# Storing the first three blocks of a layer norm + GELU kernel tile by tile instead of block by block

## The chip, the cores and the metric

One core of one Trainium2 chip. The metric is the device time of one execution in microseconds (us). A profile is of one execution; its span is some 1.7 us shorter than the execution's time.

## The reference

```python
x: (8, 1024, 2048) float32; gamma, beta: (2048,) float32; eps = 1e-5
mean = np.mean(x, axis=-1, keepdims=True)
var = np.var(x, axis=-1, keepdims=True)
normalized = (x - mean) / np.sqrt(var + eps)
out = gamma * normalized + beta
return 0.5 * out * (1 + np.tanh(np.sqrt(2 / np.pi) * (out + 0.044715 * out ** 3)))
```

67.1 MB are read and 67.1 MB written, and each element is touched once, so little can beat the rate of the transfers.

## The kernel before

The 8192 rows are 64 tiles of 128 rows (1 MB each). Block 0 is tile 0 alone; blocks 1 to 21 have three tiles (3 MB each). A block has one input buffer, there are seven, GELU writes back into it, and the block is stored from it. The load of block b + 7 is emitted behind the store of block b, because it takes the same buffer.

```python
NB = 7
starts = [0] + list(range(1, ntiles, R))                  # R = 3
def rows(ap, b):
    return ap[rows_of[b]].rearrange("(p k) d -> p k d", p=P)
def load(b):
    xt = xin.tile([P, R, d], F32, name="xt")              # pool of NB buffers
    src = rows(xf, b); m = src.shape[1]
    if b < 2:
        for k in range(m):
            nc.sync.dma_start(out=xt[:, k, :], in_=src[:, k, :])      # L68
    else:
        nc.sync.dma_start(out=xt, in_=src)                            # L70
    # ... (cut)
```

With `(p k) d`, partition p holds three rows that lie next to each other in memory. A whole block therefore moves as one run of 24 KB per partition, a single tile as one run of 8 KB.

```python
def gelu(j):
    g, k = of_tile[j]
    b, q = block_of[j]
    dst = rows(of, b)
    last = b >= len(starts) - 3
    for h, (pt, s) in enumerate(zip(ps[j % 2], halves)):
        nc.scalar.activation(out=xts[j][:, s], in_=pt, func=ACTF.Gelu_apprx_tanh,
                             scale=rstds[g][0][:, k:k + 1])           # L178
        if j == ntiles - 1:
            nc.scalar.dma_start(out=dst[:, q, s], in_=xts[j][:, s])
    if last:
        if j < ntiles - 1:
            nc.scalar.dma_start(out=dst[:, q, :], in_=xts[j])
    elif q == dst.shape[1] - 1:
        nc.scalar.dma_start(out=dst, in_=blocks[b][:, :dst.shape[1], :])
        if b + NB < len(starts):
            load(b + NB)
```

Loads are issued by SyncE (queue q1 in the profile), stores by ScalarE (queue q10), which also does the GELU, a third of the statistics and the scaled diagonals for the matrix products.

Of the kernel before, what the change touches and what calls it, by code (L numbers as in the profile page):

```python
# [19 lines left out]
def kernel(  # L20
# [10 lines left out]
    nc = tc.nc  # L31
# [3 lines left out]
    ntiles = n // P  # L35
# [12 lines left out]
    xts, blocks = {}, {}  # L48


    starts = [0] + list(range(1, ntiles, R))
# [7 lines left out]
# [4 lines that stand above are left out]
        xt = xin.tile([P, R, d], F32, name="xt")  # L63
        src = rows(xf, b)
        m = src.shape[1]
# [6 lines that stand above are left out]
            xts[starts[b] + k] = xt[:, k, :]  # L72
        blocks[b] = xt
# [98 lines left out]
    def gelu(j):  # L172
        g, k = of_tile[j]
        b, q = block_of[j]
        dst = rows(of, b)
        last = b >= len(starts) - 3
        for h, (pt, s) in enumerate(zip(ps[j % 2], halves)):
            nc.scalar.activation(out=xts[j][:, s], in_=pt, func=ACTF.Gelu_apprx_tanh,  # L178
                                 scale=rstds[g][0][:, k:k + 1])
            if j == ntiles - 1:  # L180
                nc.scalar.dma_start(out=dst[:, q, s], in_=xts[j][:, s])
        if last:
            if j < ntiles - 1:
                nc.scalar.dma_start(out=dst[:, q, :], in_=xts[j])
        elif q == dst.shape[1] - 1:
            nc.scalar.dma_start(out=dst, in_=blocks[b][:, :dst.shape[1], :])
            if b + NB < len(starts):
                load(b + NB)

# [7 lines left out]
    for j in range(ntiles):  # L197
        g, k = of_tile[j]
        target = min(len(chunks), max(pos, done_at[g] + AFTER[k]))
        while pos < target:  # L200
            i, c = chunks[pos]
            chunk(i, c)
            pos += 1
            h = of_tile[i][0]
            if done_at[h] == pos:
                while passes and of_tile[passes[0][1]][0] <= h:
                    f, q = passes.pop(0)
                    f(q)
                group_chain(h)
        if k == 0:  # L210
            for q in range(groups[g]):
                diagonal(j + q)
        affine(j)
        if j > 0:
            gelu(j - 1)
        now = of_tile[chunks[min(pos, len(chunks) - 1)][0]][0]
        if passes and of_tile[passes[0][1]][0] <= now and k != 1:
            f, q = passes.pop(0)
            f(q)
    gelu(ntiles - 1)  # L220


# [33 lines left out]
```

## Time and profile before

| | before |
|---|---|
| time, median of the first 3 runs | 319.91 us (319.67 to 320.07) |
| span of the profiled run | 317.9 us |
| busy: PE, VectorE, ScalarE | 80%, 84%, 76% |
| bytes moved, mean rate | 134.38 MB, 423 GB/s |
| transfer engines, slices 2 to 39 of 40 | 90% busy or more each |

It is read so: no compute engine is near full over the span (VectorE comes closest: 203.91 us of the middle 220), while the 16 transfer engines (DMA) are busy for 90% or more in all but the first and the last slice. The prediction below shows the lines.

### The profile page before, as it was taken

What the parts mean: (1) busy time and instruction counts of PE and PEld (TensorE: products, weight loads), DVE (VectorE), ACT (ScalarE), POOL (GpSimd) and SP (SyncE); (2) the same over time, 40 slices, a digit from 0 to 9 for tenths busy, and PEclk for the clock granted to TensorE, in tenths of its full rate; (3) what the DMA queues carried; (4) which work ended last, traced back from release to release, by engine and by line L of the source; (5) the groups of instructions that cost most, each with busy time, mean ns of one, the idle gap of its engine ahead of it and who ended that gap; (6) DMA issues with size and microseconds to landing.
All of it is one profiled execution on the core that took longest, in us unless ns stands there. A gap on an engine that the chain in (4) does not pass through costs nothing.

```text
span 317.9 us, 2209 instructions
## 1 busy us (share of the span) xinstructions
PE 255.8 (80%) x528; PEld 104.1 (33%) x528; DVE 266.1 (84%) x344; ACT 242.6 (76%) x282; POOL 91.2 (29%) x181
## 2 busy tenths in 40 slices
PE   5987979978989889789789895777979595979920
PEld 2322434323433333333233332332423232424400
DVE  2678889999999999999999979797979879797600
ACT  2365989998898988988988969587787769685720
POOL 0203324414225144043142250404234150506000
PEclk9997979999999999999999999979799998979985
DMA  7999999999999999999999999999999999999996
GB/s 292 436 442 442 387 438 422 428 429 430 436 431 433 430 433 433 427 436 431 427 433 439 430 430 432 433 431 436 424 436 433 436 425 433 430 439 409 426 429 265
DMA packets 7649, 134.38 MB, mean 423 GB/s; under 512 B 850, under 2 KB 850, under 8 KB 1106
## 3 DMA queue, kind: packets, MB, share of 16 engines
q1 hardware_dynamic: 3456, 67.11, 49.5%
q10 hardware_dynamic: 4180, 67.13, 49.3%
q8 instruction: 4, 0.07, 0.1%
q14 instruction: 9, 0.07, 0.1%
HBM read 67.13 MB, written 67.11 MB: 422 GB/s over the span
## 4 chain that ended last, share of the span: by engine, by line
DMA 42%; DVE 31%; issue 9%; POOL 5%; PE 4%; ACT 4%; ACTq 0%; POOLq 0%; DVEq 0%; SPq 0%
DMA out_dram<-xt 26%; DVE ps L166 17%; DMA xt<-in_x_dram 16%; DVE st L125 13%; PE ps L169 4%; ACT xt L178 3%; DVE mv L127 1%; POOL y L149 1%; ACT w L160 1%; POOL t L152 1%; ACT junk L131 1%; POOL ve L148 1%; POOL t L151 1%; POOL y L153 1%; POOL t L150 0%
## 5 line engine op out<-in xcount | busy, mean ns | idle before, releaser
L169 PE MATMUL ps<-b_t,w 128*128 128x512 f32 x512 | 241.8, 626 | 44.4 <-DVE ps L166 38.9
L166 DVE SCALAR_TENSOR_TENSOR ps<-xt,mv,g_t 128x1024 f32<-128x1024 f32 x128 | 156.2, 1265 | 7.0 <-ACT xt L178 6.9
L169 PEld LDWEIGHTS ps<-b_t,w 128*128 128x128 f32 x512 | 99.0, 199 | 188.0 <-issue 102.3
L178 ACT ACTIVATE xt<-ps,y 128x1024 f32<-128x1024 f32 x128 | 137.3, 1104 | 25.9 <-PE ps L169 24.9
L125 DVE BATCH_NORM_STATS2 st<-xt 128x6 f32<-128x512 f32 x172 | 107.9, 680 | 23.3 <-DMA xt<-in_x_dram 23.3
L138 POOL TENSOR_SCALAR mv<-sq 128x1 f32<-128x1 f32 x21 | 8.7, 416 | 144.5 <-ACT junk L136 144.5
L136 ACT ACTIVATE junk<-xt,mv 128x2048 fp8e5<-128x2048 f32 x21 | 42.0, 2002 | 8.0 <-ACT xt L178 8.0
L131 ACT ACTIVATE junk<-xt 128x2048 fp8e5<-128x2048 f32 x21 | 40.0, 1904 | 8.4 <-DMA xt<-in_x_dram 7.9
L149 POOL TENSOR_TENSOR y<-ve,power 128x3 f32<-128x3 f32 (+1 forms) x22 | 34.7, 1577 | 1.8
L148 POOL TENSOR_SCALAR ve<-mv 128x3 f32<-128x3 f32 (+1 forms) x22 | 20.2, 918 | 45.5 <-DVE mv L127 45.3
L160 ACT ACTIVATE w<-ident,std 128x128 f32<-128x128 f32 x64 | 20.8, 388 | 7.1 <-POOL std L154 7.1
L127 DVE BATCH_NORM_AGGREGATE mv<-st 128x2 f32<-128x24 f32 x43 | 11.3, 263 | 2.7
L98 PE MATMUL ps<-g_t,ones 1*128 1x512 f32 x8 | 7.2, 1073 | 3.7 <-DMA g_t<-in_gamma_dram 3.7
L101 ACT ACTIVATE g_t<-ps 128x1024 f32<-128x1024 f32 x2 | 2.0, 1023 | 6.7 <-PE ps L98 6.7
L98 PE MATMUL ps<-b_t,ones 1*128 1x512 f32 x8 | 7.0, 1056 | 0.0
L152 POOL TENSOR_SCALAR t<-t 128x3 f32<-128x3 f32 (+1 forms) x22 | 6.3, 287 | 1.9
L151 POOL TENSOR_TENSOR t<-t,ve 128x3 f32<-128x3 f32 (+1 forms) x22 | 6.1, 276 | 1.7
L153 POOL TENSOR_TENSOR y<-y,t 128x3 f32<-128x3 f32 (+1 forms) x22 | 5.2, 235 | 1.8
L101 ACT ACTIVATE b_t<-ps 128x1024 f32<-128x1024 f32 x2 | 2.0, 1023 | 4.8 <-PE ps L98 4.8
L150 POOL TENSOR_TENSOR t<-y 128x3 f32<-128x3 f32 (+1 forms) x22 | 5.1, 234 | 1.7
L154 POOL TENSOR_TENSOR std<-ve,y 128x3 f32<-128x3 f32 (+1 forms) x22 | 4.3, 194 | 1.7
L98 PEld LDWEIGHTS ps<-g_t,ones 1*128 1x128 f32 x8 | 2.5, 325 | 6.8 <-issue 6.8
(12 smaller groups left out, 13.0 us busy)
## 6 DMA issues: line engine op xcount, KB each, us to landing
xt<-in_x_dram SPq DMA_DIRECT2D x20, 3072.0 KB, 22.5
out_dram<-xt ACTq DMA_DIRECT2D x18, 3072.0 KB, 34.9
out_dram<-xt ACTq DMA_DIRECT2D x9, 1024.0 KB, 18.3
xt<-in_x_dram SPq DMA_DIRECT2D x4, 1024.0 KB, 8.6
out_dram<-xt ACTq DMA_DIRECT2D x2, 512.0 KB, 12.1
g_t<-in_gamma_dram ACTq DMA_DIRECT2D x1, 8.0 KB
b_t<-in_beta_dram ACTq DMA_DIRECT2D x1, 8.0 KB
```

Of the source, the lines that this page charges most:

```text
L98: nc.tensor.matmul(pt[:, c:c + BANK], lhsT=ones[0:1, :], rhs=row[0:1, s.start + c:s.start + c + BANK], start=True, stop=True)
L125: nc.vector.bn_stats(out=sts[i][:, c, :], in_=xts[i][:, c * BANK:(c + 1) * BANK])
L127: nc.vector.bn_aggr(out=slot(i), in_=sts.pop(i))
L131: nc.scalar.activation(out=junk, in_=xts[i], func=ACTF.Identity, scale=-1.0 / d, accum_out=slot(i)[:, 0:1], saturate=False)
L136: nc.scalar.activation(out=junk, in_=xts[i], func=ACTF.Square, bias=slot(i)[:, 0:1], accum_out=sq, saturate=False)
L148: po.tensor_scalar(out=ve, in0=mvs[g][:, :, 1], scalar1=float(eps), scalar2=None, op0=ADD)
L149: po.tensor_tensor(out=y, in0=ve, in1=power[:, :m], op=mybir.AluOpType.pow)
L152: po.tensor_scalar(out=t, in0=t, scalar1=-0.5, scalar2=1.5, op0=MUL, op1=ADD)
L160: nc.scalar.activation(out=w, in_=ident, func=ACTF.Identity, scale=rstds[g][1][:, k:k + 1])
L166: nc.vector.scalar_tensor_tensor(out=pt, in0=xts[j][:, s], scalar=mvs[g][:, k, 0:1], in1=g_t[:, s], op0=ADD if j in on_scalar else SUB, op ...
L169: nc.tensor.matmul(pt[:, c:c + BANK], lhsT=wts[j], rhs=b_t[:, s.start + c:s.start + c + BANK], start=False, stop=True, skip_group_check=True)
L178: nc.scalar.activation(out=xts[j][:, s], in_=pt, func=ACTF.Gelu_apprx_tanh, scale=rstds[g][0][:, k:k + 1])
```

## The change: intent and diff

The whole-block store of block 1 cannot leave before its third tile is done, at about 44 us. Single tiles can leave from about 35 us on. The intent is an earlier start of the stores, and with it buffers that come free earlier.

```diff
-        last = b >= len(starts) - 3
+        single = not 3 <= b < len(starts) - 3
...
-        if last:
-            if j < ntiles - 1:
-                nc.scalar.dma_start(out=dst[:, q, :], in_=xts[j])
-        elif q == dst.shape[1] - 1:
-            nc.scalar.dma_start(out=dst, in_=blocks[b][:, :dst.shape[1], :])
+        if single and j < ntiles - 1:
+            nc.scalar.dma_start(out=dst[:, q, :], in_=xts[j])
+        if q == dst.shape[1] - 1:
+            if not single:
+                nc.scalar.dma_start(out=dst, in_=blocks[b][:, :dst.shape[1], :])
             if b + NB < len(starts):
                 load(b + NB)
```

(In the last three blocks `b + NB` is past the end, so the load's new place changes nothing there.)

## The prediction

> **What bounds the kernel now.** I read the head of the page first: the slices of the span, then the time of DMA issues to landing.
>
> ```profile
> span 317.9 us, 2209 instructions
> ...
> DMA  7999999999999999999999999999999999999996
> GB/s 292 436 442 442 387 438 422 428 429 430 436 431 433 430 433 433 427 436 431 427 433 439 430 430 432 433 431 436 424 436 433 436 425 433 430 439 409 426 429 265
> DMA packets 7649, 134.38 MB, mean 423 GB/s; under 512 B 850, under 2 KB 850, under 8 KB 1106
> ...
> xt<-in_x_dram SPq DMA_DIRECT2D x20, 3072.0 KB, 22.5
> out_dram<-xt ACTq DMA_DIRECT2D x18, 3072.0 KB, 34.9
> ```
>
> The transfers are busy 90% or more in every slice but the first and the last. A 3 MB store takes a median 34.9 us to land, though 3.15 MB at 432 GB/s is 7.3 us alone and 14.6 us when it shares the engines half and half. So the median store stands some 20 us in line behind other stores. VectorE is busy 84% of the span and ScalarE 76%; both work ahead of the stores.
>
> Second, the windows of the span (columns: window, length, busy us of five engines with counts, clock, DMA share, GB/s).
>
> ```profile
> 0.00:4.00 4.00, 0.33 (x1) 0.36 (x2) 0.17 (x1) 1.49 (x2) 0.54 (x6) 1.00 0.49 164
> 8.00:30.00 22.00, 18.65 (x24) 7.00 (x23) 16.19 (x25) 10.67 (x14) 5.21 (x15) 0.96 1.03 441
> 30.00:34.00 4.00, 4.00 (x8) 1.62 (x7) 2.89 (x5) 3.54 (x5) 0.00 (x0) 0.78 1.02 393
> 34.00:38.00 4.00, 4.00 (x11) 1.72 (x10) 4.00 (x6) 4.00 (x5) 1.16 (x3) 1.00 0.96 410
> 48.00:52.00 4.00, 4.00 (x11) 1.82 (x10) 3.95 (x5) 3.33 (x5) 3.00 (x6) 1.00 0.95 406
> 60.00:280.00 220.00, 182.94 (x398) 74.61 (x396) 203.91 (x266) 184.94 (x218) 71.09 (x135) 0.98 1.00 432
> 312.00:318.00 6.00, 0.00 (x0) 0.00 (x0) 0.00 (x0) 0.00 (x0) 0.00 (x0) 0.50 0.51 208
> ```
>
> For 220 us in the middle 432 GB/s flow, at a DMA share of 1.00. The span is then nearly a sum: 134.38 MB / 432 GB/s = 311.1 us; the head (first 4 us at 164 GB/s) loses 4 x (1 - 164/432) = 2.5 us; the tail (last 6 us at 208) loses 3.1 us. That is 316.7 of 317.9 us. Where the stores begin, between 30 and 52 us, there are small dips: 4 x (1 - 393/432) = 0.36, 4 x (1 - 410/432) = 0.20 and 4 x (1 - 406/432) = 0.24 us, some 0.8 us in all. That is all that this change could fill, as it acts from about 34 us on.
>
> Third, how loads and stores share the engines. Two windows of the DMA queues: q1 is the load queue, q10 the store queue (packets, MB, share). The first has the 1 MB store of tile 0 beside 3 MB loads, the second only 3 MB transfers.
>
> ```profile
> DMA packets 192, 3.02 MB, mean 432 GB/s; under 512 B 15, under 2 KB 15, under 8 KB 15
> ...
> q1 hardware_dynamic: 96, 2.36, 78.2%
> q10 hardware_dynamic: 96, 0.66, 22.5%
> ```
>
> ```profile
> q10 hardware_dynamic: 494, 10.81, 50.3%
> q1 hardware_dynamic: 485, 10.74, 49.9%
> ```
>
> Packets alternate one for one in both (96 to 96; 494 to 485). A row of a block is one packet of 24 KB, a row of a single tile one of 8 KB, so a single tile's store beside block loads gets a quarter of the bytes, and the sum still reaches 432 GB/s.
>
> Fourth, the chain that ended last and the waits of the load queue.
>
> ```profile
> 209.48 44.87 DMA out_dram<-xt
> 254.37 0.03 SPq L70
> 254.40 0.03 issue
> 254.43 22.49 DMA xt<-in_x_dram
> ```
>
> ```profile
> SPq L70 <- DMA out_dram<-xt: 237.3, 15, 33.8
> ...
> SPq L70 <- DMA xt<-in_x_dram: 6.4, 2, 4.3
> ```
>
> A load goes out when the store of the block seven before it has landed: 15 waits, 237.3 us. A slot comes free only as fast as stores drain, and they drain at the rate of the DMA engines.
>
> **What the Trainium skill says.** In "DMA: Bandwidth & Descriptors", section "Queues, rings and completion order", each DMA engine goes round-robin between the queues that have work, packet by packet. The trace agrees: 96 packets against 96, 2.36 MB against 0.66. The same page, section "Issuing engines are not separate DMA queues", says that transfers started from different engines run on the same 16 DMA engines and interleave; here the pure loads from 8 to 30 us make 441 GB/s and the mixed stretch 432, so starting stores sooner takes the bytes from loads. Its section "Where 436 GB/s comes from" puts the ceiling at 435 GB/s; 432 leaves nothing to win. And "Rules for kernel authors" asks for at least 1 MiB in a transfer, which single tiles still have.
>
> **The change part by part.** Removed: the two 3 MB stores of blocks 1 and 2. Added: six 1 MB stores, so four issues more on ScalarE's queue. Bytes: the same. Tile 0 was stored alone already; the last three blocks are unchanged; the test for the load is only moved in the text, and it still waits for all of a block's stores.
>
> ```profile
> 32.51 2.10 ACT L178 ACTIVATE xt<-ps,y 128x1024 f32<-128x1024 f32 x2
> ...
> 36.48 2.11 ACT L178 ACTIVATE xt<-ps,y 128x1024 f32<-128x1024 f32 x2
> ...
> 42.37 2.09 ACT L178 ACTIVATE xt<-ps,y 128x1024 f32<-128x1024 f32 x2
> 44.49 0.37 ACTq L186 DMA_DIRECT2D out_dram<-xt  x1
> 44.92 2.00 ACT L136 ACTIVATE junk<-xt,mv 128x2048 fp8e5<-128x2048 f32 x1 [0.45 <-ACT xt L178]
> ```
>
> These are the three tiles of block 1. Its first two tiles now go out at about 34.7 and 39 us, ten and six us ahead of the block's issue at 44.49. An issue leaves ScalarE idle 0.45 us, so four more cost 4 x 0.45 = 1.8 us of ScalarE between 34 and 57 us. This lies beside the transfers.
>
> What the early issue brings, worked out with the shares above. From the timeline, tile 0's store goes out at 30.17 us and the load that waits for it at 45.53; 1.05 MB in 15.4 us shows the quarter share. Until about 45 us the store queue is busy with tile 0 before and after, and tiles 1 and 2 only stand behind it. At 45 us some 6.3 MB of loads are left (the last prefetched block and the one just issued; my count of load packets to that time). At three quarters of 432, 324 GB/s, they take 19.4 us, to about 64.5 us. In that time the stores move 19.4 x 108 = 2.1 MB: tiles 1 and 2 and nothing of tile 3. Then the load queue is dry, tile 3 goes at full rate in 2.4 us, to 67 us, and with a landing of about 2 us the next load is issued at 67 to 69 us. Before, it was at 65.6. So the slot comes free no earlier, rather 1 to 3 us later, while the loads are ahead by about 7 us of theirs. The store queue then holds tiles 4 to 6 (issued by 57 us, 3.1 MB, 7.3 us alone), which cover the pause until loads flow again at about 72 us. The next load (before: 80.0 us) follows at 80 to 83 us, and the cadence of 14.5 us, two times 3.15 MB at 432, is back.
>
> Sum: bytes 0; dips between 44 and 52 us, now mixed without a break, -0.2; two new changes between pure and mixed traffic, +0.1 to +0.3; 64 more completion packets (4 transfers of 16), nothing visible; ScalarE's 1.8 us, hidden. Together 0.0 us, give or take 0.5.
>
> **The rivals.** (a) Earlier stores fill the start and free slots sooner. For it: all dips lie there. Against: they sum to 0.8 us, and the engines already run at 393 to 441 GB/s then. It makes 319.1 us at best. (b) The quarter share keeps slots waiting and, with the load queue dry from 64 to 72 us, the store queue dries too. For it: the store queue is short so early. Against: 4.2 MB of stores are issued and undone at 64 us, 9.7 us at full rate, against a pause of 7 to 8 us. If it fails, 1 to 3 us without transfers: 321 to 323. (c) The issues hold ScalarE. In the waits, the load queue waited 6.4 us for earlier loads, so an issue can stand behind an older transfer; stores in quick succession might hold ScalarE some us in the same way, and VectorE behind it. Against: the line of stores that builds up, some 20 us, must first be eaten up, and the last 512 KB stores land 12.1 us after their issue where 1.2 us would move them. So it costs 0 us, or 1.8 if I have the slack wrong: 321.7.
>
> **Range and chances.** The main case leaves the median where it is, 319.8 us (319.91 with -0.1 for the dips). The three runs before lie within 0.4 us. Rival (a) sets the low side and some of (b) the high: 318.9 to 321.0. Two per cent would be 6.4 us, eight times the dips, or twice the worst of (b): faster 0.01, slower 0.02, same 0.97.
>
> **What would show it.** Right: the middle 220 us again at 432 GB/s and a DMA share of 1.00; in the DMA queues between 46 and 62 us equal packets and some 75% to 25% of the share; the load queue empty and only stores for several us after 64; the load of the block after next issued at 67 to 69 us and not before 65; ScalarE's four added idle pieces without a mark in the end. Wrong: a slice after the second with a DMA digit under 9, loads issued well before 65.6 us, stores of 8 KB rows running at half share beside loads, or a 3 MB-store time to landing that falls near 15 us, which would mean that the store line is gone and the compute sets the end.

## The result, and the profile after

| | before | after |
|---|---|---|
| median of 6 runs | 319.81 us (319.66 to 320.38) | 319.91 us (319.79 to 320.33) |
| ratio | | 1.0002, 95% interval 0.9989 to 1.0015 |

A ratio is the mean time of one kernel's runs over that of the other's runs of the same rounds, so it is not quite the ratio of the medians. Executions over 1.5% slower than the fastest of the same kernel are left out of the means. The time is the same.

The head of the page of the changed kernel, and its times from issue to landing:

```profile
span 318.1 us, 2217 instructions
...
DMA  7999999999999999999999999999999999999996
GB/s 296 450 426 436 390 427 429 437 411 442 437 431 426 423 442 436 420 430 440 430 433 426 436 436 433 420 436 439 430 426 436 436 431 426 430 436 413 426 429 263
DMA packets 8225, 134.38 MB, mean 422 GB/s; under 512 B 914, under 2 KB 914, under 8 KB 1170
...
xt<-in_x_dram SPq DMA_DIRECT2D x20, 3072.0 KB, 23.8
out_dram<-xt ACTq DMA_DIRECT2D x16, 3072.0 KB, 37.6
out_dram<-xt ACTq DMA_DIRECT2D x15, 1024.0 KB, 20.9
```

The bytes are the same and the same slices are full. There are 576 packets more (8225 against 7649): 512 because each of the 128 partition rows of two blocks became three, and 64 completions (4 transfers of 16). A 3 MB store still stands in line for most of its 37.6 us. The long middle window of the changed kernel runs at the same rate:

```profile
60.00:280.00 220.00, 184.78 (x396) 75.65 (x395) 203.44 (x264) 183.31 (x214) 72.00 (x136) 0.96 1.01 432
```

Now the start, where the change acts. ScalarE's timeline of the changed kernel (start, length, engine and line; in brackets the idle time before):

```profile
34.70 0.37 ACTq L184 DMA_DIRECT2D out_dram<-xt  x1
35.11 2.00 ACT L136 ACTIVATE junk<-xt,mv 128x2048 fp8e5<-128x2048 f32 x1 [0.45 <-ACT xt L179]
...
39.24 0.34 ACTq L184 DMA_DIRECT2D out_dram<-xt  x1
39.63 1.91 ACT L131 ACTIVATE junk<-xt 128x2048 fp8e5<-128x2048 f32 x1 [0.42 <-ACT xt L179]
```

The first two tiles of block 1 do leave at 34.7 and 39.2 us, ten and five us before the whole block did. What they then get of the engines is in the DMA queues from 46 to 62 us, first of the kernel before, then of the changed kernel (packets, MB, share of the engines):

```profile
q1 hardware_dynamic: 166, 3.69, 55.8%
q10 hardware_dynamic: 131, 3.15, 45.7%
```

```profile
q1 hardware_dynamic: 231, 5.26, 76.6%
q10 hardware_dynamic: 223, 1.70, 25.0%
```

In the changed kernel the packets are again one for one (231 to 223), but the stores' are a third of the size, so they move 1.70 MB where they moved 3.15. The loads gain what the stores lose: 5.26 MB for 3.69. Then, from 64 to 72 us, the loads of the changed kernel have run dry:

```profile
DMA packets 468, 3.34 MB, mean 418 GB/s; under 512 B 63, under 2 KB 63, under 8 KB 63
...
q10 hardware_dynamic: 451, 3.30, 97.7%
q1 hardware_dynamic: 16, 0.02, 0.8%
```

97.7% of the engines go to stores: there were enough of them in line to fill the gap, at 418 GB/s. Over the first 64 us as a whole the queues moved this, before and after:

```profile
q1 hardware_dynamic: 1370, 21.74, 81.1%
q10 hardware_dynamic: 303, 4.51, 16.6%
```

```profile
q1 hardware_dynamic: 1424, 23.04, 85.7%
q10 hardware_dynamic: 437, 3.20, 11.9%
```

The sum is the same, 26.28 and 26.26 MB. Loads gained 1.30 MB and stores lost 1.31, although two of three stores were issued sooner; by 90 us each queue is back within 0.1 MB of the kernel before. Last, the issue of the two loads that wait for blocks 1 and 2, in SyncE's timeline, before and after:

```profile
65.63 0.33 SPq L70 DMA_DIRECT2D xt<-in_x_dram  x1
...
80.01 0.33 SPq L70 DMA_DIRECT2D xt<-in_x_dram  x1
```

```profile
68.18 0.33 SPq L70 DMA_DIRECT2D xt<-in_x_dram  x1
...
83.47 0.33 SPq L70 DMA_DIRECT2D xt<-in_x_dram  x1
```

The buffers come free 2.6 and 3.5 us *later* than before, although the first two tiles of each block left earlier. (The last tile, which frees the buffer, leaves no sooner than the whole block did: at 45.12 us for 44.49, and at 57.55 for 56.71.)

### The profile page after: what moved, and what is told of

Same layout as the page of the kernel before. It is cut to its first block, busy times and chain, and to the rows that moved or that the text cites. A ratio compares the mean times of both kernels' runs of the same rounds, so it can differ in the third digit from the quotient of the medians.

```text
span 318.1 us, 2217 instructions
## 1 busy us (share of the span) xinstructions
PE 256.9 (81%) x528; PEld 104.6 (33%) x528; DVE 266.2 (84%) x344; ACT 242.7 (76%) x282; POOL 91.3 (29%) x181
## 2 busy tenths in 40 slices
DMA packets 8225, 134.38 MB, mean 422 GB/s; under 512 B 914, under 2 KB 914, under 8 KB 1170
## 4 chain that ended last, share of the span: by engine, by line
DMA 42%; DVE 31%; issue 9%; POOL 5%; PE 4%; ACT 4%; ACTq 0%; POOLq 0%; DVEq 0%; SPq 0%
DMA out_dram<-xt 26%; DMA xt<-in_x_dram 17%; DVE ps L166 17%; DVE st L125 13%; PE ps L169 4%; ACT xt L179 3%; DVE mv L127 1%; POOL y L149 1%; POOL t L151 1%; ACT w L160 1%; ACT junk L131 1%; POOL t L150 1%; POOL ve L148 1%; POOL t L152 0%; POOL y L153 0%
## 5 line engine op out<-in xcount | busy, mean ns | idle before, releaser
L179 ACT ACTIVATE xt<-ps,y 128x1024 f32<-128x1024 f32 x128 | 137.2, 1104 | 26.5 <-PE ps L169 24.7
L131 ACT ACTIVATE junk<-xt 128x2048 fp8e5<-128x2048 f32 x21 | 40.0, 1905 | 8.3 <-DMA xt<-in_x_dram 6.6
L149 POOL TENSOR_TENSOR y<-ve,power 128x3 f32<-128x3 f32 (+1 forms) x22 | 33.8, 1537 | 1.8
L151 POOL TENSOR_TENSOR t<-t,ve 128x3 f32<-128x3 f32 (+1 forms) x22 | 7.9, 361 | 1.7
L150 POOL TENSOR_TENSOR t<-y 128x3 f32<-128x3 f32 (+1 forms) x22 | 6.8, 310 | 1.7
L152 POOL TENSOR_SCALAR t<-t 128x3 f32<-128x3 f32 (+1 forms) x22 | 4.3, 197 | 1.9
L153 POOL TENSOR_TENSOR y<-y,t 128x3 f32<-128x3 f32 (+1 forms) x22 | 4.3, 195 | 1.8
## 6 DMA issues: line engine op xcount, KB each, us to landing
out_dram<-xt ACTq DMA_DIRECT2D x16, 3072.0 KB, 37.6
```

Source lines behind the costliest of these rows:

```text
L131: nc.scalar.activation(out=junk, in_=xts[i], func=ACTF.Identity, scale=-1.0 / d, accum_out=slot(i)[:, 0:1], saturate=False)
L149: po.tensor_tensor(out=y, in0=ve, in1=power[:, :m], op=mybir.AluOpType.pow)
L151: po.tensor_tensor(out=t, in0=t, in1=ve, op=MUL)
```

## The experiments

Twelve kernels ran; "the kernel before" was run again beside each. The theory to test (A): the transfer engines are full from 8 us on, so earlier stores only take bytes from loads, and a line of stores covers what ScalarE loses. The first rival (B): a gain and a loss are both there and cancel by chance. Others came up on the way. By the rule that a change under 2% counts as the same, e2, e9 and e12 below are the same as the kernel before and e11 is unclear; where I call one slower all the same, its 95% interval leaves out 1.

### Each block's part alone

```diff
-        single = not 3 <= b < len(starts) - 3
+        single = not 2 <= b < len(starts) - 3            # e3: blocks 0 and 1
+        single = b in (0, 2) or b >= len(starts) - 3     # e4: blocks 0 and 2
```

> Blocks 0 and 1 tile by tile, block 2 whole again. Theory A: the load that waits for block 1's store is issued at 67 to 69 us as in the changed kernel (quarter share until the loads run dry), the next one at about 80 to 82 us in place of the changed kernel's 83.5, for block 2's rows of 24 KB then share half and half; total 319 to 321 us.

> Block 1 whole, block 2 tile by tile. Theory A: the load that waits for block 1's store goes out at 65 to 66 us as in the kernel before, the next one later than that kernel's 80.0, at 83 to 90 us, since block 2's 8 KB rows then have a quarter share beside two loads; total 319 to 321 us.

One run each (state unknown): 319.81 and 320.14 us, beside 319.87 of the kernel before. SyncE's timelines, of e3 and then of e4:

```profile
67.99 0.33 SPq L70 DMA_DIRECT2D xt<-in_x_dram  x1
...
78.88 0.33 SPq L70 DMA_DIRECT2D xt<-in_x_dram  x1
```

```profile
64.76 0.33 SPq L70 DMA_DIRECT2D xt<-in_x_dram  x1
...
83.40 0.33 SPq L70 DMA_DIRECT2D xt<-in_x_dram  x1
```

Each delay belongs to the block that was made single, and only to it: block 1 single gives 68.0 us for the first load, block 2 single 83.4 for the second. Two of the four times lie outside the forecast, by 1.1 us (78.9 for 80 to 82) and 0.2 us (64.8 for 65 to 66), both to the early side.

### The quarter share taken away

```diff
-        if b < 2:
+        if b < 2 or 5 <= b <= 8:          # load(): these blocks, too, tile by tile
```

> The changed kernel, but the loads of blocks 5 to 8, those that run beside the single-tile stores, also go tile by tile, so both queues have packets of 8 KB and share half and half. Theory A: the load that waits for block 1's store is issued earlier than the changed kernel's 68.2 us, at about 57 to 62, and the total stays at 319.9 within 0.5%. Rival B (the late slot costs something that the early store wins back): with the late slot cured the gain shows, 317 to 319 us.

321.05 us (320.45 to 321.87), ratio 1.0037 (1.0025 to 1.0049). SyncE's timeline of this run:

```profile
55.30 1.62 SPq L68 DMA_DIRECT2D xt<-in_x_dram  x2
```

The two issues in it go out at 55.30 and, by the record of the single instructions, 56.59 us; the second is the first tile of the load that waits for block 1, 11.6 us before the changed kernel's 68.18 and just ahead of the forecast (57 to 62). (The other two tiles of that load go out at 66.3 and 66.7 us.) From 40 to 56 us the two queues now share half and half, 50.2% and 50.6%. So the short rows beside long ones did delay the buffer: with rows of the same length the delay is gone. But the time does not fall, it rises by 0.4%, which lies inside the forecast of 0.5%. Rival B, which wanted 317 to 319, is not borne out; as this run has a cost of its own, the stronger evidence against B is the equal sum of bytes in the first 64 us above. Where the cost comes from is shown only in part: between 30 and 40 us 378 GB/s flow in this run, 406 in the changed kernel, worth 10 x (406 - 378)/432 = 0.65 us. A second candidate, whose effect on the end is not shown: ScalarE issued the last store of block 2 at 61.5 us, not at 57.6 as in the changed kernel. That store signals its completion on a semaphore (a counter on which engines wait) that a load issued at 40.9 us also uses, and it went out when that load had landed (at 61.4 us). This kind of wait comes back below.

### Where the transfer engines do have idle time: four buffers

```diff
-    NB = 7
+    NB = 4          # e5 in the kernel before, e6 in the changed kernel
```

> The kernel before with four input buffers in place of seven, the base for the next run. The prefetch then ends at about 28 us and the DMA engines must wait for slots: transfers idle in the first 60 us, and a slot's cycle (load, wait, compute, store, landing) of some 60 to 70 us over four slots gives 15 to 17.5 us a block: 330 to 375 us.

> The changed kernel with four buffers. Theory A (the change is worth nothing only because the DMA engines have no idle time to fill at the start): here they have, single tiles meet no loads and land at once, so block 1's slot comes free some 5 us sooner and the time falls by 1 to 6 us against the four-buffer kernel before. Rival D (earlier issue is worth nothing in itself, as the slot always waits for the last tile): the same within 1 us.

e5: 397.36 us (396.31 to 398.74), more than the 330 to 375 expected; I had taken a buffer's cycle for too short: from 72.81 to 347.00 us a block took 18.3 us, not 15 to 17.5. e6: 394.46 us (392.03 to 395.23). Against the kernel before of the same rounds the ratios are 1.2422 (1.2390 to 1.2453) and 1.2316 (1.2275 to 1.2357): the change wins 0.9% here, and no run of one overlaps a run of the other. (The profiled run of e6, 392.03 us, is its fastest.) The window from 30 to 60 us of e5, then of e6:

```profile
30.00:60.00 30.00, 25.46 (x57) 10.41 (x56) 26.95 (x35) 27.68 (x33) 8.22 (x17) 0.99 0.80 309
```

```profile
30.00:60.00 30.00, 25.19 (x56) 10.26 (x55) 26.43 (x34) 26.49 (x32) 7.96 (x17) 0.98 0.92 364
```

With four buffers the transfer engines are busy for 0.80 of this stretch before the change and 0.92 after: early tiles fill idle time when there is some. SyncE's timeline shows what becomes of it, e5 first, then e6 (the loads that wait for blocks 1 and 2, and the last load):

```profile
53.67 0.33 SPq L70 DMA_DIRECT2D xt<-in_x_dram  x1
...
72.81 0.33 SPq L70 DMA_DIRECT2D xt<-in_x_dram  x1
...
347.00 0.33 SPq L70 DMA_DIRECT2D xt<-in_x_dram  x1
```

```profile
52.46 0.33 SPq L70 DMA_DIRECT2D xt<-in_x_dram  x1
...
68.50 0.33 SPq L70 DMA_DIRECT2D xt<-in_x_dram  x1
...
342.81 0.33 SPq L70 DMA_DIRECT2D xt<-in_x_dram  x1
```

Block 2's buffer comes free 4.3 us sooner, and the last load still goes out 4.2 us sooner. (I had expected the gain at block 1, which gives 1.2.) So the change is not worthless in itself: with seven buffers it has nothing to fill.

### Where compute sets the end: half stores

```diff
-    nc.scalar.dma_start(out=dst, in_=blocks[b][:, :dst.shape[1], :])
+    nc.scalar.dma_start(out=dst[:, :, :H], in_=blocks[b][:, :dst.shape[1], :H])   # blocks 3 to 18
```

This leaves half of those blocks' output unwritten, a wrong result. (The line is e8's; e7's edit does the same for blocks 3 to 18.) e7 is the kernel before with it, e8 the changed kernel.

> The kernel before, but blocks 3 to 18 store only the left half of their columns (a wrong result on purpose), which takes 25 MB or 58 us from the DMA engines, so that compute sets the end. VectorE's 12.47 us a group from 48 us on puts the last issue some 10 us sooner: 299 to 303 us. It is the base for the next run.

> The changed kernel with the same half stores (wrong result on purpose). Theory A with the hidden cost as predicted: ScalarE's four issues of 0.42 us, 1.7 us, are no longer covered by the line of stores and show in part, 0.5 to 2 us slower than the half-store kernel before. Rival C (they cost nothing even there, since ScalarE is not the bound): the same within 0.3 us. Rival B: faster, by 1 us or more, from the earlier start.

e7: 296.22 us (295.95 to 296.47), under the 299 to 303 expected, ratio 0.9255 (0.9240 to 0.9271). e8: 297.05 us (296.83 to 297.06), ratio 0.9282 (0.9269 to 0.9296). The changed kernel is 0.8 us slower; the runs do not overlap, the intervals touch. In the middle of e7 VectorE is busy 207.66 of 210 us and the transfers have room (0.91):

```profile
60.00:270.00 210.00, 181.97 (x406) 73.96 (x404) 207.66 (x271) 184.31 (x219) 77.37 (x135) 1.00 0.91 369
```

That is the hidden cost of the four added issues. ScalarE loses 4 x 0.42 = 1.7 us, and half of it reaches the end when compute sets it. In the two traces GELU lags by 0.5 us in e8 once the four issues are past, at 64 us, and its last piece still does (290.13 for 289.67 us). In the real kernel it lies behind the line of stores.

### The change carried to every block

```diff
-        single = not 3 <= b < len(starts) - 3
+        single = True
```

> Every block is stored tile by tile: 36 more issues in all than the changed kernel has over its own blocks 3 to 18 (48 stores of 1 MB in place of 16 of 3 MB). Theory A (the 16 DMA engines are the bound from 8 us to the last stores, so the order and the size of the transfers only share out the same 432 GB/s): 319.9 us, within 0.5%, a DMA share of 1.00 in the middle, although the loads run at three quarters of the bytes while a store is beside them and then pause for several us in each block. Rival B (gain of earlier stores and cost of slots freed later cancel in the changed kernel by chance): the two do not cancel when repeated 16 times, so the time moves by 3 us or more, either way. Rival C (ScalarE's issue time counts): 32 more issues x 0.42 us = 13 us of ScalarE; if a third of it shows, 324 us.

338.89 us (337.60 to 341.37), ratio 1.0616 (1.0579 to 1.0652). Theory A, as I had put it ("the order and the size of the transfers only share out the same rate"), falls: transfers of the same bytes can cost 19 us. (B had asked for 3 us or more here and got it in number, but the traces below show other effects than B's two.) ScalarE's waits for transfers in this run:

```profile
ACT junk L136 <- DMA out_dram<-xt: 19.6, 7, 3.8
ACT xt L179 <- DMA xt<-in_x_dram: 18.1, 2, 11.6
...
ACT xt L179 <- DMA out_dram<-xt: 3.2, 1, 3.2
ACT junk L131 <- DMA xt<-in_x_dram: 2.7, 1, 2.7
ACT junk L131 <- DMA out_dram<-xt: 0.9, 1, 0.9
```

44.5 us together, with the 0.4 us of each issue, where the changed kernel has 6.6 (its own wait for data). GELU (L179) works on a tile that is long in its buffer, so it needs none of these transfers. Its longest wait, in ScalarE's timeline, and SyncE's timeline shortly before:

```profile
252.02 2.10 ACT L179 ACTIVATE xt<-ps,y 128x1024 f32<-128x1024 f32 x2
265.28 0.34 ACTq L184 DMA_DIRECT2D out_dram<-xt  x1
265.72 1.11 ACT L179 ACTIVATE xt<-ps,y 128x1024 f32<-128x1024 f32 x1 [11.60 <-DMA xt<-in_x_dram]
```

```profile
249.60 0.33 SPq L70 DMA_DIRECT2D xt<-in_x_dram  x1
```

The tile is done at 254.1 us, but its store goes out at 265.28. In the instruction records all transfers of the program signal on eight completion semaphores, which are given out in turn. The store at 265.28 has number 99, and so has the load of 249.60; just ahead of the store stands a wait on that very semaphore, which ends at 265.2. So the store waited for an unrelated load, and everything behind it on ScalarE with it. By the same records all twelve of these waits are of this kind, and the changed kernel has none. With 65 stores in place of 33 (32 more, not the 36 of the expectation), such meetings are frequent.

Two windows of the same run show the rest:

```profile
60.00:270.00 210.00, 156.39 (x327) 62.51 (x325) 172.23 (x222) 150.61 (x175) 53.65 (x112) 0.94 1.01 422
290.00:334.00 44.00, 36.58 (x83) 14.92 (x81) 33.79 (x40) 34.07 (x40) 12.90 (x23) 1.00 0.71 291
```

Up to 270 us the engines are full but move 422 GB/s, not 432. From 290 us on the line of stores is gone and the transfers wait for compute (0.71); in the last 12 us the packet records show all 16 engines at work or none. Both cost time: the first 210 x (1 - 422/432) = 4.9 us, most of the rest is compute that came late. I had three explanations left: ScalarE's issue time (C), its standing behind older transfers (E), and the transfer engines themselves with short rows (F).

### Telling the three apart

e9 gives ScalarE the time of the issues without any transfer:

```diff
+        if not single and q < 2:
+            for _ in range(2):
+                nc.scalar.activation(out=tiny, in_=ones[:, 0:1], func=ACTF.Gelu_apprx_tanh)
```

> The changed kernel with 64 tiny activations (one element per partition, about 0.2 us each as the one in the prologue) after the first two tiles of each of blocks 3 to 18: about 13 us of ScalarE more, the size of the 32 issues that the all-single kernel added, but no transfer more. Theory E (the all-single kernel lost its 19 us by ScalarE standing behind older transfers whose semaphore its next store uses, with 8 semaphores for all transfers): 319.5 to 321.5 us. Rival C (ScalarE's issue time): 327 us or more.

320.35 us (319.73 to 321.28), ratio 1.0013 (0.9992 to 1.0034). ScalarE is busy 251.2 us, for 242.7 in the changed kernel: 8.5 us more, not the 13 that I meant. By rival C, with e1's 19 us for 13, that should cost 12 us; it costs 0.4. Rival C falls: ScalarE's time alone vanishes behind the line of stores.

e10 stores blocks 3 to 18 as two tiles and one, e11 has nine single blocks:

```diff
+        if not single and q == 1:                                                   # e10
+            nc.scalar.dma_start(out=dst[:, :2, :], in_=blocks[b][:, :2, :])
-                nc.scalar.dma_start(out=dst, in_=blocks[b][:, :dst.shape[1], :])
+                nc.scalar.dma_start(out=dst[:, 2, :], in_=xts[j])
-        single = not 3 <= b < len(starts) - 3
+        single = not 9 <= b < len(starts) - 3                                       # e11
```

> Blocks 3 to 18 are stored as two tiles and one tile, 16 issues more than the changed kernel where the all-single kernel had 32. Theory E: in flight in the middle are some 37.6/14.5 x 2 = 5.2 stores and 1.6 loads, under 8, so ScalarE waits little for transfers (under 10 us against that kernel's 44 us in its waits), and the time is 319.5 to 323 us. Rival C (cost in proportion to the issues): half of 19 us, 329 us. Rival F (rows shorter than the loads' 24 KB cost rate, as the 420 GB/s of that kernel's middle hints): about 322 to 324 us with few waits.

> The change carried three times as far: blocks 0 to 8 tile by tile. Theory E with the slack of the store line: ScalarE loses some 10 to 20 us to issues and waits by 130 us, which eats most of the line of some 20 us but does not go through it: 319.5 to 322 us, with a 3 MB store's time to landing well under the changed kernel's 37.6 us. If loss were in proportion to the blocks made single (6 of the 16 that cost 19 us): 327 us.

e10: 328.65 us (327.27 to 329.43), ratio 1.0265 (1.0237 to 1.0293). e11: 326.94 us (324.02 to 327.85), ratio 1.0191 (1.0135 to 1.0246). Both are misses for E as I had put it. Both hit the forecasts of a loss in proportion to the added stores (329 and 327 us): e1, e10 and e11 lose 0.59, 0.54 and 0.58 us for each of 32, 16 and 12. Why the price is so even stays open; ScalarE's issue time is not it (e9), and the traces show different losses. In e10 I had expected under 10 us of such waits; there are 42.4:

```profile
ACT junk L136 <- DMA xt<-in_x_dram: 37.9, 11, 5.2
...
ACT junk L131 <- DMA out_dram<-xt: 4.5, 1, 4.5
```

Counting transfers in flight was the wrong measure: a semaphore comes round in a fixed turn, and a store meets whatever holds its number, here mostly the latest load, however few are in flight in all. In e11 there are four such waits, 15.6 us in all (9.0 before GELU's line, 6.6 of the 8.9 before L131), the last at 142 us. They did not reach the end by way of idle transfers: the engines' share is 1.01 from 60 to 270 us and 0.99 from 270 to 316. The windows from 60 to 270 us of e10 and of e11, and the last 8 us of e11's transfers:

```profile
60.00:270.00 210.00, 166.29 (x346) 66.01 (x345) 178.69 (x230) 158.41 (x188) 56.19 (x115) 0.95 1.01 424
```

```profile
60.00:270.00 210.00, 175.03 (x370) 71.73 (x369) 190.74 (x245) 171.06 (x201) 63.94 (x128) 0.93 1.01 427
316.50:324.50 8.00, 0.00 (x0) 0.00 (x0) 0.00 (x0) 0.00 (x0) 0.00 (x0) 0.51 0.15 62
```

The rate is lower again while the engines are full, and at e11's end most of the 16 engines are done while, by the packet records, one works alone from about 322 to 324.5 us. The 16 engines had come apart. (In e10 they had not: there the share is 0.79 and 0.62 in the last two stretches of 10 us, 300 to 320, and in the end all 16 stop and start together, as in e1.) In the changed kernel the last engine is done at 316.6 us, 2.5 us after the first. This points to F, so the last run asks for it alone: as many issues as the changed kernel, 3 MB each, but in rows of 8 KB.

```diff
-                nc.scalar.dma_start(out=dst, in_=blocks[b][:, :dst.shape[1], :])
+                nc.scalar.dma_start(out=of[rows_of[b]].rearrange("(k p) d -> p k d", p=P), in_=blocks[b])
```

> The changed kernel with as many issues as it has, but the whole-block stores of blocks 3 to 18 go out in rows of 8 KB in place of 24 KB (each block's three tiles land in swapped rows of the output: a wrong result on purpose). Theory E (the loss of the all-single kernel is ScalarE's standing behind older transfers, which comes with the number of transfers): no such waits, 432 GB/s or nearly in the middle, 319.5 to 321.5 us. Theory F (the loss is the transfer engines' own: rows of 8 KB beside rows of 24 KB lower the rate or set the 16 engines apart): 420 to 427 GB/s in the middle, or a last store that lands many us after its issue, and 323 to 330 us with ScalarE waiting for no transfer.

324.45 us (322.73 to 326.91), ratio 1.0161 (1.0129 to 1.0192), rows swapped. ScalarE waits for no transfer but its own data (6.3 us). Its window from 60 to 270 us, and the transfers' end:

```profile
60.00:270.00 210.00, 177.68 (x381) 72.25 (x380) 198.49 (x257) 179.13 (x211) 66.43 (x129) 0.96 1.01 428
315.70:319.70 4.00, 0.00 (x0) 0.00 (x0) 0.00 (x0) 0.00 (x0) 0.00 (x0) 0.50 0.20 82
```

So with no store added and no such wait, the short rows of 16 blocks cost 1.6%. Whether it takes the loads' long rows beside them, no run tests. The profiled run is the fastest of the six (322.73 us). It shows a rate of 428, worth 210 x (1 - 428/432) = 1.9 us, and a long end. How the rest of the 5 us of the median comes about, and why the runs differ by 4 us, no profile here shows. The swapped rows also lie elsewhere in memory, which I could not take apart from their length. Of e1's 19 us, then, some 5 go with short rows (if e12 carries over) and the rest fits the late compute that the semaphore waits bring; that split is argued, not shown, because no run takes those waits away while it keeps the transfers.

## Why the prediction was right

- **"The transfers are the bound, so bytes over rate give the time."** Right for this change: 432 GB/s over the middle 220 us before and after, the same full slices, ratio 1.0002. The first 64 us move 26.28 and 26.26 MB. As a general rule it was too wide: e1, e10, e11 and e12 move the same bytes and take 1.6 to 6.2% longer. One reading beside it was loose: the 441 GB/s of the pure loads, above the ceiling that it cites, comes with a share of 1.03 (a window counts a packet's whole time where it starts), and 441/1.03 is 428. So pure loads are not shown to be faster than mixed traffic.
- **"A single tile's store beside block loads gets a quarter of the bytes."** Right: 25.0% and 76.6% between 46 and 62 us; e2, with equal rows, took the effect away.
- **"The slot comes free no earlier, rather 1 to 3 us later."** Right: 68.18 for 65.63 (forecast 67 to 69), and step by step: by the packet records tile 3 was moved by 66.8 us (forecast 67). Its landing took 1.3 us more; the 2 us of the forecast stand on no line shown. The second was forecast at 80 to 83 and came at 83.47. The reason for the half microsecond: block 2's last tile met the next load and went packet for packet with it again (76 to 82 packets from 72 to 78 us, of 8 and 24 KB), which the working had left out.
- **"The load queue is dry from 64 to 72 us, and the stores in line cover it."** Right: 97.7% of the engines on stores, 418 GB/s.
- **"Dips between 44 and 52 us, -0.2."** Wrong, and small: from 44 to 52 us the rate is 419 before and 418 after. The dip that I saw from 48 to 52 us followed four microseconds at 432; I had read a fluctuation of a short window as a loss.
- **"ScalarE's 1.8 us, hidden."** Right: 0.42 to 0.45 us an issue; e8 shows 0.8 us of it once compute sets the end, and e9 hides five times as much.
- **Rival (c), "an issue can stand behind an older transfer".** It did not matter in this change (no store of the changed kernel waited so), but it is real: e1 has 44.5 us of it.

## What to carry to other kernels

Where the transfer engines are full, an earlier store wins nothing: it takes its bytes from the loads, and a buffer that is freed by the last tile of a block is freed no sooner. Test an "earlier" change by asking what is idle at that moment; with four buffers something was, and the same edit won 0.9%. And don't carry a harmless edit on without measuring: two more blocks in short stores cost nothing, eight cost 1.9%, all of them 6.2%.

## What the Trainium skill lacked or had wrong

- "DMA: Bandwidth & Descriptors", "Queues, rings and completion order": it tells the round-robin by packet, and the trace agrees, but not what follows for the bytes. Here a packet is one row's run, so the queue with 8 KB rows gets 25.0% beside 24 KB rows (231 to 223 packets, 5.26 to 1.70 MB).
- The same page, "Rules for kernel authors", asks for at least 1 MiB in a transfer for full bandwidth. Size alone does not settle it here: 3 MiB stores in 8 KB rows beside 24 KB loads took 1.6% longer, at 428 for 432 GB/s in the middle (the rows also lay elsewhere in memory), and 1 MiB stores in all blocks ran at 422.
- The same page, "Why a DMA increments its semaphore by 16 and not by 1" (and "Dedicate one sem" in the rules): it warns of wrong data when two transfers in flight share one, not of time. Here a program's transfers share eight in turn, and an issue waited for the older holder: 44.5 us of ScalarE in e1, where the changed kernel had 6.6 us.
- "Issuing engines are not separate DMA queues" calls the issue time "usually small". No page gives the gap that an issue leaves on a ScalarE that computes: 0.42 to 0.45 us each here.
- Pages know of single engines that are slower than others; none gives how far the 16 can come apart over a kernel: in e11 they finished over 8 us (share 0.15 from 316.5 to 324.5 us), in the changed kernel over 2.5.
